# One buffer for the transposed rows, routing factors written twice, and routing weights applied by pairs of token groups

## The chip, the cores and the metric

The kernel runs on one core of one Trainium2 chip. The metric is the device time of one execution in microseconds (us), as the median of several runs.

## What is computed

The reference runs two blocks, one after the other, on 256 tokens of width 1024. The change touches only the last layer of the second block, a mixture of 16,384 tiny experts, and the buffer in which transposed rows are kept for all the large products. Cut to what matters, the layer is:

```
def _peer(h, w_q, subkeys, w_down, w_up):          # h: tokens x 1024
    q = h @ w_q                                    # 8 heads x 2 halves x 128
    s = q . subkeys                                # scores of 128 + 128 half keys for each head
    v, i = top_k(s, 16)                            # the best 16 of each half
    tv, tj = top_k(v0 + v1, 16)                    # the best 16 of the 256 sums
    eidx = 128 * i0 + i1                           # expert number of each choice
    w = softmax(tv)
    a = gelu(h . w_down[eidx])                     # one number per token and chosen expert
    return sum over choices of (w * a) * w_up[eidx]
```

The layer chooses 8 x 16 = 128 experts for each token. Everything is float32.

## The kernel before

Nothing is gathered. The kernel computes all 16,384 expert values for all 256 tokens by dense products, multiplies them with a matrix that holds the routing weight where an expert was chosen and zero elsewhere, and multiplies the result with all of `w_up`. An expert number is 128 * i0 + i1; the i0 from 0 to 63 make the first half (tile `Ga`, called G2 in the code) and those from 64 to 127 the second (tile `Gb`, G1). In both, i1 lies across the partitions.

Products in full precision are made of three passes in a reduced 32-bit form: each operand is split into a high and a low part (`wsplit`: ScalarE, ACT, casts `raw` to `whi`, L239; VectorE, DVE, subtracts to get `wlo`, L240), and `mm3` issues high x high (L244), high x low (L245) and low x high (L246). Weights come in tiles of 128 x 1024, 0.5 MB, through SP's DMA queue, into five `raw` buffers and three pairs of `whi` and `wlo`. The transposed, normalised rows of the tokens, h, stand as a high and a low part of 8 x 256 columns in two buffers, `bh` and `bl` of 2064 elements a partition each (`big_hl`): the high part from element 16 of `bh`, the low part from element 0 of `bl`. Each of four users (two input projections, one merge, the last layer) gets a new generation of them. In the last stage their space is used again for split rows of expert values (`uph` in `bl`, `upl` in `bh`, eight slots).

The last layer runs in this order. PE (TensorE) takes its instructions in the order in which they were written out, as does each other engine.

1. Queries, scores and the top-16 searches (`routing`, `route`), spread between the first products by `drain`. `route(t)` ends, for each tile of 128 tokens, with three transposes and the writing of the factors: `ije` (i0 and i1 for each choice and token) and `wpt` (high and low part of the weight), as 16-bit numbers, 256 tokens wide.
2. First `down` half: 32 calls of `down`, each with two weight tiles of 24 passes of 256 columns, and a gelu by ACT (L1168) into `Ga`.
3. Second `down` half: 32 calls into `Gb`; meanwhile `Ga` is multiplied with the routing weights, 8 tokens (a group) at a time, 32 groups.
4. First `up` half: 64 calls of `upc` on `Ga`, each with 12 passes of 512 columns (L1219); meanwhile `Gb` is multiplied with its routing weights, 32 groups.
5. Second `up` half: 64 calls on `Gb`, without weighing, then the end: residual, norm, output.

A group is prepared on DVE by `make`: R (128 choices x 128 values of i1 for each of 8 tokens, one where equal, L1180), E (the same for 64 values of i0, L1182), and two L (E times high and low part of the weight, L1185). R and L stand in one of two buffers, RL0 and RL1. `weigh` then runs 16 matmuls of 64 columns on PE (two for each token, L1199), which make the dense matrix of weights of that group in PSUM, and DVE multiplies it into the expert values (L1201). `ready` calls `make` for a later group; the loops call `ready` for the next group and then `weigh` for the present one, `spread` over the calls of `down` and `upc`. In R, E and L tokens are interleaved by two, so that the two tokens of a pair lie in adjacent elements: `iota2` holds each number twice, and a matmul reads every second element.

Of the kernel before, what the change touches and what calls it, by code (L numbers as in the profile page):

```python
# [8 lines left out]
F32R = mybir.dt.float32r  # L9
# [161 lines left out]
def _body(ctx, tc, ins, out, dbg, stop):  # L171
# [3 lines left out]
    const = ctx.enter_context(tc.tile_pool(name="const", bufs=1))  # L175
    keep = ctx.enter_context(tc.tile_pool(name="keep", bufs=1))
    raw = ctx.enter_context(tc.tile_pool(name="raw", bufs=5))
    hl = ctx.enter_context(tc.tile_pool(name="hl", bufs=3))
    small = ctx.enter_context(tc.tile_pool(name="small", bufs=4))

# [155 lines left out]
    x2d = [dram.tile([128, 1024], F32, name=f"x2d{t}") for t in range(2)]  # L336
    mod2 = keep.tile([128, 48], F32, name="mod2")
    both = []
    with ExitStack() as c1:
        k1 = c1.enter_context(tc.tile_pool(name="k1", bufs=1))  # L340
        w1 = c1.enter_context(tc.tile_pool(name="w1", bufs=2))
# [17 lines left out]

        def big_hl():  # L360

            both[:] = [keep.tile([128, 2064], F32R, name=n, tag=n) for n in ("bh", "bl")]
            return [m[:, o:o + 2048].rearrange("p (k n) -> p k n", k=8) for m, o in zip(both, (16, 0))]

        scr = k1.tile([128, 256], BF, name="scr")
        scr2 = k1.tile([128, 1024], BF, name="scr2")
# [668 lines left out]
                T.matmul(sp[:, t, f], qhs[h % 2][:, f, t * 128:(t + 1) * 128], sub[:, 2 * h + f], start=True, stop=True)  # L1035
        S.copy(sco[:, h], sp)

    iota2 = k2.tile([128, 128, 2], HF, name="iota2")
    V.tensor_copy(iota2, K["iota"][:, :, None].to_broadcast([128, 128, 2]))
    cst, dst, io16 = [cut([16], HF) for _ in range(3)]  # L1040
    for m, n in ((cst, K["cst"]), (dst, K["dst"]), (io16, K["iota"][:, :16])):
        V.tensor_copy(m, n)
    ge, pr = cut([8, 16, 16], HF), cut([8, 16, 16], HF)
    ije = k2.tile([128, 2, 256], HF, name="ije")
    wpt = k2.tile([128, 2, 256], HF, name="wpt")

    def route(t):

        V.tensor_copy(idf[:, t], idx[:, t])
        v, ix = val[:, t], idf[:, t]  # L1050
        cand = cut([8, NCAND])
        o = 0
        for i0, ni, nj in CAND:
            V.tensor_tensor(cand[:, :, o:o + ni * nj].rearrange("p h (i j) -> p h i j", j=nj),
                            v[:, :, 0, i0:i0 + ni, None].to_broadcast([128, 8, ni, nj]),
                            v[:, :, 1, None, 0:nj].to_broadcast([128, 8, ni, nj]), op=OP.add)
            o += ni * nj
        yield 1.2
        tv, st = [cut([8, 16]) for _ in range(2)]
        pf, d0 = [cut([8, 16], HF) for _ in range(2)]  # L1060
        tp = cut([8, 16], U32)
        wia = cut([3, 8, 16])
        for h in range(8):
            top16(tv[:, h], tp[:, h], cand[:, h], NCAND)
            yield 1.0
        V.tensor_copy(pf, tp)
        V.tensor_sub(st, tv, tv[:, :, 0:1].to_broadcast([128, 8, 16]))
        S.activation(tv, st, AF.Exp)
        V.tensor_copy(d0[:, :, 0:1], ix[:, :, 0, 0:1])
        V.tensor_sub(d0[:, :, 1:], ix[:, :, 0, 1:], ix[:, :, 0, :15])  # L1070
        sh4 = [128, 8, 16, 16]
        f2 = lambda m: m.rearrange("p h s -> p (h s)")
        col = lambda m: f2(m)[:, :, None].to_broadcast([128, 128, 16])
        row = lambda m: m[:, None, :].to_broadcast([128, 128, 16])
        f3 = lambda m: m.rearrange("p h s i -> p (h s) i")
        V.tensor_tensor(f3(ge), col(pf), row(cst), op=OP.is_ge)
        yield 2.8
        sm = small.tile([128, 8], F32, name="sm8")
        V.tensor_reduce(sm, tv, axis=AX.X, op=OP.add)
        V.reciprocal(sm, sm)  # L1080
        V.tensor_mul(wia[:, 0], tv, sm[:, :, None].to_broadcast([128, 8, 16]))
        V.tensor_mul(pr, ge, d0[:, :, None, :].to_broadcast(sh4))
        yield 1.7
        V.tensor_reduce(wia[:, 1], pr, axis=AX.X, op=OP.add)
        yield 2.2
        V.tensor_mul(f3(pr), f3(ge), row(dst))
        yield 1.2
        V.tensor_reduce(st, pr, axis=AX.X, op=OP.add)
        V.tensor_sub(st, pf, st)
        yield 2.4  # L1090
        V.tensor_tensor(f3(ge), col(st), row(io16), op=OP.is_equal)
        yield 2.2
        V.tensor_mul(pr, ge, ix[:, :, 1, None, :].to_broadcast(sh4))
        yield 1.2
        V.tensor_reduce(wia[:, 2], pr, axis=AX.X, op=OP.add)
        yield 2.2
        ps = pb.tile([128, 3, 128], F32, name="tp")
        for i in range(3):
            T.transpose(ps[:, i], wia[:, i].rearrange("p h s -> p (h s)"), ident)
        ts = slice(t * 128, t * 128 + 128)  # L1100
        S.copy(ije[:, :, ts], ps[:, 1:3])
        rem = cut([128])
        S.mul(rem, ps[:, 0], UPSCALE)
        V.tensor_copy(wpt[:, 0, ts], rem)
        V.tensor_sub(wpt[:, 1, ts], rem, wpt[:, 0, ts])
        yield 0.5

    done, budget = [0], [0.0]
# [59 lines left out]
        S.activation(Gh[:, 2 * (c % 32):2 * (c % 32) + 2], ps, AF.Gelu_apprx_tanh)  # L1168

    ng = 8  # L1170
    pair = lambda m, t: m[:, t:t + ng].rearrange("p (a b) -> p a b", b=2)[:, :, None, :]

    def make(hf, t):

        R, L = RL(nth[0] % 2)
        nth[0] += 1
        R = R.rearrange("p (a i b) -> p a i b", a=ng // 2, b=2)
        L = L.rearrange("p (q a i b) -> p q a i b", q=2, a=ng // 2, b=2)
        E = w2.tile([128, ng // 2, 64, 2], HF, name="E", bufs=2)
        V.tensor_tensor(R, iota2[:, None].to_broadcast([128, ng // 2, 128, 2]),  # L1180
                        pair(ije[:, 1], t).to_broadcast([128, ng // 2, 128, 2]), op=OP.is_equal)
        V.tensor_tensor(E, iota2[:, None, hf * 64:hf * 64 + 64].to_broadcast([128, ng // 2, 64, 2]),  # L1182
                        pair(ije[:, 0], t).to_broadcast([128, ng // 2, 64, 2]), op=OP.is_equal)
        for p in range(2):
            V.tensor_tensor(L[:, p], E, pair(wpt[:, p], t).to_broadcast([128, ng // 2, 64, 2]), op=OP.mult)  # L1185
        return R, L

    ahead = []
# [4 lines left out]
    def weigh(Gh):  # L1193

        hf, t, R, L = ahead.pop(0)
        ps = pb.tile([128, ng, 64], F32, name="tp")
        for i in range(ng):
            for p in range(2):
                T.matmul(ps[:, i], R[:, i // 2, :, i % 2], L[:, p, i // 2, :, i % 2], start=p == 0, stop=p == 1)  # L1199
        gv = Gh[:, :, t:t + ng]  # L1200
        V.tensor_mul(gv, gv, ps.rearrange("p t i -> p i t"))  # L1201

# [29 lines left out]
    G1 = k2.tile([128, 64, 256], F32, name="Gb", tag="G1")  # L1232
    two = [w2.tile([128, 2, 1024], HF, name=f"RL{i}") for i in range(2)]
    RL = lambda i: (two[i][:, 0], two[i][:, 1])
    ready(0, 0)
    for c in range(32):
        down(G1, 32 + c)
        for g in spread(32, c, 30) if c < 30 else ():
            if g < 31:
                ready(0, ng * (g + 1))  # L1240
            weigh(G2)
    uph, upl = [m[:, o:o + 2048].rearrange("p (k n) -> p k n", k=8) for m, o in zip(both, (0, 16))]
    ready(1, 0)
    for c in range(64):
        upc(G2, c)
        for g in spread(32, c, 62) if c < 62 else ():
            if g < 31:
                ready(1, ng * (g + 1))
            weigh(G1)
    rs = k2.tile([128, 64 * 256], F32, name="rs2", tag="G2")  # L1250
    used[0] = 0
    xo = cut([2, 1024])
# [61 lines left out]
```

## Time and profile before

| | us |
|---|---|
| median of 3 runs | 1245.26 (1244.03 to 1246.6) |
| the profiled execution | 1246.62 |
| its span, first to last instruction | 1244.8 |
| PE busy | 1190.5 (96%) |
| DVE busy | 959.2 (77%) |
| ACT busy | 585.6 (47%) |

Busy time of PE is made of matmuls that overlap: the next starts while one is still draining, so their durations add up to more than the span, and how fast PE really works is read from the starts of successive matmuls. PEld is the loading of the stationary operand, which runs beside them. In the views, `pa` are the accumulators of `down`, `up` those of `upc`, `tp` the matrix of weights, `RL` the two buffers of R and L, `bh` and `bl` the rows. In square brackets stands the time for which an engine was idle before an instruction, and what ended it.

### The profile page before, as it was taken

The page shows a single profiled execution, that of the slowest core. Times are in us where ns is not written, and L with a number is a line of the kernel's source. Part 1 is how long each engine was busy: PE and PEld are TensorE (multiplying, and loading weights), DVE is VectorE, ACT ScalarE, POOL GpSimd, SP SyncE. Part 2 cuts the span into 40 slices and gives each one's busy share as a digit, 9 for nine tenths or more (in the row PEclk, how much of TensorE's full clock was granted, in tenths as well). Part 3 has the DMA queues.
Part 4 walks back from the last instruction along what each step waited for, and adds up shares of the span by engine and source line. Part 5 has one row for each costly group of instructions (what it writes and reads, how often), then busy time and mean ns, then how long its engine had stood idle before and what let it go on. Part 6 is the DMA issues. An engine that isn't in the chain of part 4 may idle for free. (4 is left out here: it accounts for less than half of the span.)

```text
span 1244.8 us, 22791 instructions
## 1 busy us (share of the span) xinstructions
PE 1190.5 (96%) x8960; PEld 1071.1 (86%) x8960; DVE 959.2 (77%) x2015; ACT 585.6 (47%) x907; POOL 8.7 (1%) x14
## 2 busy tenths in 40 slices
PE   3999999899999899899999999999999999999996
PEld 2998899778788799899999999998777777888884
DVE  6879869768798789997546778778888887666555
ACT  3445547323553545454544444445444444555553
POOL 0000000000000000000000000000000000000001
PEclk9999999999999999999999999999999999999998
DMA  9999846287373444556565555555555556777551
GB/s 320 363 323 317 284 163 198 92 287 253 103 238 118 170 143 165 169 171 202 190 195 175 170 170 170 170 169 171 169 172 179 173 172 237 227 230 238 183 186 51
DMA packets 67451, 245.22 MB, mean 197 GB/s; under 512 B 7504, under 2 KB 8032, under 8 KB 67088
## 3 DMA queue, kind: packets, MB, share of 16 engines
q1 hardware_dynamic: 65136, 236.34, 57.7%
q10 hardware_dynamic: 1440, 4.20, 0.9%
q0 software_dynamic: 768, 3.23, 0.8%
q8 instruction: 70, 1.15, 0.4%
q14 instruction: 37, 0.30, 0.1%
HBM read 241.11 MB, written 2.62 MB: 196 GB/s over the span
## 5 line engine op out<-in xcount | busy, mean ns | idle before, releaser
L240 DVE TENSOR_TENSOR wlo<-raw,whi 128x1024 fp32r<-128x1024 f32 x351 | 427.9, 1222 | 121.8 <-ACT whi L239 120.7
L239 ACT CAST whi<-raw 128x1024 fp32r<-128x1024 f32 x351 | 368.0, 1050 | 326.4 <-PE pa L245 221.7
L246 PE MATMUL pa<-bh,wlo 128*128 128x256 f32 x1120 | 314.6, 281 | 3.7 <-DVE wlo L240 3.5
L244 PE MATMUL pa<-bh,whi 128*128 128x256 f32 x1120 | 317.2, 283 | 0.0
L245 PE MATMUL pa<-bl,whi 128*128 128x256 f32 x1120 | 313.9, 280 | 0.0
L246 PEld LDWEIGHTS pa<-bh,wlo 128*128 128x128 f32 x1120 | 211.7, 189 | 5.0 <-DVE wlo L240 4.9
L245 PEld LDWEIGHTS pa<-bl,whi 128*128 128x128 f32 x1120 | 214.5, 192 | 0.0
L244 PEld LDWEIGHTS pa<-bh,whi 128*128 128x128 f32 x1120 | 211.8, 189 | 0.0
L1219 PE MATMUL up<-whi,bh 128*128 128x512 f32 x508 | 164.1, 403 | 0.0
L1219 PE MATMUL up<-wlo,bh 128*128 128x512 f32 x508 | 160.1, 394 | 0.0
L1219 PE MATMUL up<-whi,bl 128*128 128x512 f32 x508 | 159.8, 394 | 0.0
L1219 PEld LDWEIGHTS up<-wlo,bh 128*128 128x128 f32 x508 | 95.4, 188 | 23.5 <-DVE wlo L240 0.3
L1219 PEld LDWEIGHTS up<-whi,bl 128*128 128x128 f32 x508 | 95.4, 188 | 22.3
L244 PE MATMUL mm<-whi,bh 128*128 128x256 f32 x352 | 102.2, 290 | 11.0 <-ACT whi L239 8.2
L1219 PEld LDWEIGHTS up<-whi,bh 128*128 128x128 f32 x508 | 93.4, 189 | 19.3 <-ACT whi L239 0.2
L245 PE MATMUL mm<-wlo,bh 128*128 128x256 f32 x352 | 101.2, 288 | 2.1 <-DVE wlo L240 2.1
L246 PE MATMUL mm<-whi,bl 128*128 128x256 f32 x352 | 101.1, 287 | 1.1 <-DVE bl L332 1.0
L1185 DVE TENSOR_TENSOR RL<-E,wpt 128x512 f16<-128x512 f16 x128 | 53.9, 422 | 33.7 <-PE tp L1199 33.7
L244 PEld LDWEIGHTS mm<-whi,bh 128*128 128x128 f32 x352 | 67.8, 193 | 13.1 <-ACT whi L239 8.6
L245 PEld LDWEIGHTS mm<-wlo,bh 128*128 128x128 f32 x352 | 67.7, 192 | 3.2 <-DVE wlo L240 2.5
L246 PEld LDWEIGHTS mm<-whi,bl 128*128 128x128 f32 x352 | 67.7, 192 | 2.3 <-DVE bl L332 1.7
L231 ACT CAST bh<-Ga 128x256 fp32r<-128x256 f32 x64 | 25.4, 406 | 86.3 <-PE up L1219 85.1
(400 smaller groups left out, 1709.7 us busy)
## 6 DMA issues: line engine op xcount, KB each, us to landing
raw<-in_wdT_dram SPq DMA_DIRECT2D x128, 512.0 KB, 3.4
raw<-in_wu_dram SPq DMA_DIRECT2D x128, 512.0 KB, 3.5
raw<-in_wada_dram SPq DMA_DIRECT2D x72, 512.0 KB, 4.8
raw<-in_win_dram SPq DMA_DIRECT2D x26, 512.0 KB, 4.5
raw<-in_win1t_dram SPq DMA_DIRECT2D x24, 512.0 KB, 5.0
raw<-in_win1n_dram SPq DMA_DIRECT2D x16, 512.0 KB, 5.2
raw<-in_wout_dram SPq DMA_DIRECT2D x16, 512.0 KB, 3.6
raw<-in_wq_dram SPq DMA_DIRECT2D x12, 512.0 KB, 3.6
```

The source lines that it names most:

```text
L231: S.copy(hi, src)
L239: S.copy(hi, t)
L240: (E or eng()).tensor_tensor(lo, t, hi, op=OP.subtract)
L244: T.matmul(o, a[0], b[0], start=first, stop=False, **kw)
L245: T.matmul(o, a[0], b[1], start=False, stop=False, **kw)
L246: T.matmul(o, a[1], b[0], start=False, stop=last, **kw)
L1185: V.tensor_tensor(L[:, p], E, pair(wpt[:, p], t).to_broadcast([128, ng // 2, 64, 2]), op=OP.mult)
L1219: T.matmul(up[t][d], s_[:, ts], v_[:, d], start=ia == 0 and n == 0, stop=ia == 127 and n == 2)
```

## The change

1. `bh` and `bl` become one buffer of 4128 elements in a pool of its own, `rowp`, which is allocated after `raw` and ahead of the `whi` and `wlo` buffers. h stands in it from element 16 on (high part, then low part), `uph` and `upl` from element 32 on.
2. `ije` and `wpt` hold each value twice, in adjacent elements. `route` writes them with two casts of `ije`, two copies of the high part by ACT, and one subtraction of twice the length on DVE; a cast on DVE goes. `iota2` becomes `iotah`, each number once. R, E and L have each token's values in adjacent elements, and the weigh matmuls read them without a stride. The doubled factors give DVE two adjacent equal elements where there were two tokens. E has one buffer, not two.
3. Two groups are prepared ahead of each loop. Then `pair` weighs two groups in a row and prepares the next two; 16 pairs are spread over the calls where 32 single weighings were.

```diff
+    rowp = ctx.enter_context(tc.tile_pool(name="rowp", bufs=1))
...
+    def parts(o):
+        return [both[0][:, i:i + 2048].rearrange("p (k n) -> p k n", k=8) for i in (o, o + 2048)]
...
-            both[:] = [keep.tile([128, 2064], F32R, name=n, tag=n) for n in ("bh", "bl")]
-            return [m[:, o:o + 2048].rearrange("p (k n) -> p k n", k=8) for m, o in zip(both, (16, 0))]
+            both[:] = [rowp.tile([128, 4128], F32R, name="bhl", tag="bhl")]
+            return parts(16)
...
-    iota2 = k2.tile([128, 128, 2], HF, name="iota2")
-    V.tensor_copy(iota2, K["iota"][:, :, None].to_broadcast([128, 128, 2]))
+    iotah = k2.tile([128, 128], HF, name="iotah")
+    V.tensor_copy(iotah, K["iota"])
...
-    ije = k2.tile([128, 2, 256], HF, name="ije")
-    wpt = k2.tile([128, 2, 256], HF, name="wpt")
+    ije = k2.tile([128, 2, 256, 2], HF, name="ije")
+    wpt = k2.tile([128, 2, 256, 2], HF, name="wpt")
...
-        S.copy(ije[:, :, ts], ps[:, 1:3])
         rem = cut([128])
         S.mul(rem, ps[:, 0], UPSCALE)
-        V.tensor_copy(wpt[:, 0, ts], rem)
-        V.tensor_sub(wpt[:, 1, ts], rem, wpt[:, 0, ts])
+        for b in range(2):
+            S.copy(ije[:, :, ts, b], ps[:, 1:3])
+            S.copy(wpt[:, 0, ts, b], rem)
+        V.tensor_sub(wpt[:, 1, ts], rem[:, :, None].to_broadcast([128, 128, 2]), wpt[:, 0, ts])
...
-    pair = lambda m, t: m[:, t:t + ng].rearrange("p (a b) -> p a b", b=2)[:, :, None, :]
+    twice = lambda m, t, w: m[:, t:t + ng, None, :].to_broadcast([128, ng, w // 2, 2])
...
-        R = R.rearrange("p (a i b) -> p a i b", a=ng // 2, b=2)
-        L = L.rearrange("p (q a i b) -> p q a i b", q=2, a=ng // 2, b=2)
-        E = w2.tile([128, ng // 2, 64, 2], HF, name="E", bufs=2)
-        V.tensor_tensor(R, iota2[:, None].to_broadcast([128, ng // 2, 128, 2]),
-                        pair(ije[:, 1], t).to_broadcast([128, ng // 2, 128, 2]), op=OP.is_equal)
-        V.tensor_tensor(E, iota2[:, None, hf * 64:hf * 64 + 64].to_broadcast([128, ng // 2, 64, 2]),
-                        pair(ije[:, 0], t).to_broadcast([128, ng // 2, 64, 2]), op=OP.is_equal)
+        two_ = lambda m: m.rearrange("p t (i b) -> p t i b", b=2)
+        R = R.rearrange("p (t i) -> p t i", t=ng)
+        L = L.rearrange("p (q t i) -> p q t i", q=2, t=ng)
+        E = w2.tile([128, ng, 64], HF, name="E")
+        V.tensor_tensor(two_(R), two_(iotah[:, None].to_broadcast([128, ng, 128])), twice(ije[:, 1], t, 128), op=OP.is_equal)
+        V.tensor_tensor(two_(E), two_(iotah[:, None, hf * 64:hf * 64 + 64].to_broadcast([128, ng, 64])),
+                        twice(ije[:, 0], t, 64), op=OP.is_equal)
         for p in range(2):
-            V.tensor_tensor(L[:, p], E, pair(wpt[:, p], t).to_broadcast([128, ng // 2, 64, 2]), op=OP.mult)
+            V.tensor_tensor(two_(L[:, p]), two_(E), twice(wpt[:, p], t, 64), op=OP.mult)
...
-                T.matmul(ps[:, i], R[:, i // 2, :, i % 2], L[:, p, i // 2, :, i % 2], start=p == 0, stop=p == 1)
+                T.matmul(ps[:, i], R[:, i], L[:, p, i], start=p == 0, stop=p == 1)
...
-    ready(0, 0)
+    def pair(Gh, hf, n):
+        for _ in range(2):
+            weigh(Gh)
+        for g in (n + 2, n + 3):
+            if g < 32:
+                ready(hf, ng * g)
+    for g in range(2):
+        ready(0, ng * g)
     for c in range(32):
         down(G1, 32 + c)
-        for g in spread(32, c, 30) if c < 30 else ():
-            if g < 31:
-                ready(0, ng * (g + 1))
-            weigh(G2)
-    uph, upl = [m[:, o:o + 2048].rearrange("p (k n) -> p k n", k=8) for m, o in zip(both, (0, 16))]
-    ready(1, 0)
+        for n in spread(16, c, 30) if c < 30 else ():
+            pair(G2, 0, 2 * n)
+    uph, upl = parts(32)
+    for g in range(2):
+        ready(1, ng * g)
     for c in range(64):
         upc(G2, c)
-        for g in spread(32, c, 62) if c < 62 else ():
-            if g < 31:
-                ready(1, ng * (g + 1))
-            weigh(G1)
+        for n in spread(16, c, 62) if c < 62 else ():
+            pair(G1, 1, 2 * n)
```

## Rows read from the trace of the kernel before

**Rows 1.** The page: busy us of PE, share of the span, instructions.
```profile
PE 1190.5 (96%) x8960; PEld 1071.1 (86%) x8960; DVE 959.2 (77%) x2015; ACT 585.6 (47%) x907; POOL 8.7 (1%) x14
```

**Rows 2.** Busy time by stretch: second `down` half, then first `up` half.
```profile
657.00:855.40 198.40, 198.40 (x2052) 197.09 (x2051) 149.13 (x226) 84.73 (x102) 0.00 (x0) 1.00 0.55 171
855.40:1049.30 193.90, 193.90 (x1270) 154.70 (x1269) 167.44 (x279) 92.19 (x130) 2.10 (x4) 1.00 0.56 182
```

**Rows 3.** PE in order of time (start, length): one `down` between two single weighings.
```profile
669.48 0.28 PE L245 MATMUL pa<-bl,whi 128*128 128x256 f32 x1
...
674.78 0.28 PE L245 MATMUL pa<-bl,whi 128*128 128x256 f32 x1
...
675.02 0.66 PE L1199 MATMUL tp<-RL 128*128 128x64 f16 x16
675.51 0.36 PE L244 MATMUL pa<-bh,whi 128*128 128x256 f32 x1
675.71 0.28 PE L245 MATMUL pa<-bl,whi 128*128 128x256 f32 x1
```

**Rows 4.** PE in order of time: two weighings in a row, and the `down` behind.
```profile
749.82 1.14 PE L1199 MATMUL tp<-RL 128*128 128x64 f16 x32
750.79 0.36 PE L244 MATMUL pa<-bh,whi 128*128 128x256 f32 x1
751.00 0.28 PE L245 MATMUL pa<-bl,whi 128*128 128x256 f32 x1
...
756.11 0.28 PE L245 MATMUL pa<-bl,whi 128*128 128x256 f32 x1
```

**Rows 5.** PE by line (count, busy us, mean ns): 669.6-749.6, 763.0-844.0, 751.0-762.3, 844.9-855.2.
```profile
L245 PE MATMUL pa<-bl,whi 128*128 128x256 f32 x208 | 58.4, 281 | 0.0
...
L246 PE MATMUL pa<-bh,wlo 128*128 128x256 f32 x208 | 58.4, 281 | 0.0
...
L245 PE MATMUL pa<-bl,whi 128*128 128x256 f32 x32 | 8.8, 276 | 0.0
...
L245 PE MATMUL pa<-bl,whi 128*128 128x256 f32 x31 | 8.6, 276 | 0.0
```

**Rows 6.** ACT in order of time: two gelus in a row, first `down` half.
```profile
652.71 0.59 ACT L1168 ACTIVATE Ga<-pa 128x512 f32<-128x512 f32 x1
...
658.15 0.59 ACT L1168 ACTIVATE Ga<-pa 128x512 f32<-128x512 f32 x1
```

**Rows 7.** PE in order of time: `up` with weighings, then two plain calls.
```profile
867.12 0.66 PE L1199 MATMUL tp<-RL 128*128 128x64 f16 x16
...
873.27 0.66 PE L1199 MATMUL tp<-RL 128*128 128x64 f16 x16
...
1091.31 0.64 PE L1219 MATMUL up<-whi,bh 128*128 128x512 f32 x2
...
1094.11 0.64 PE L1219 MATMUL up<-whi,bh 128*128 128x512 f32 x2
```

**Rows 8.** DVE in order of time, around the double weighing.
```profile
750.48 0.43 DVE L1185 TENSOR_TENSOR RL<-E,wpt 128x512 f16<-128x512 f16 x1 [1.10 <-PE tp L1199]
750.83 0.68 DVE L1201 TENSOR_TENSOR Ga<-Ga,tp 128x512 f32<-128x512 f32 x1
751.42 0.69 DVE L1180 TENSOR_TENSOR RL<-iota,ije 128x1024 f16<-128x1024 f16 x1
...
754.23 2.36 DVE L240 TENSOR_TENSOR wlo<-raw,whi 128x1024 fp32r<-128x1024 f32 x2
756.51 0.76 DVE L1182 TENSOR_TENSOR E<-iota,ije 128x512 f16<-128x512 f16 x2
```

**Rows 9.** DVE in order of time, first `up` half.
```profile
867.39 0.42 DVE L232 TENSOR_TENSOR bl<-Ga,bh 128x256 fp32r<-128x256 f32 x1 [0.56 <-PE up L1219]
```

**Rows 10.** ACT in order of time, end of `route` for the first tile.
```profile
598.35 0.29 ACT L1103 ACTIVATE rs<-tp 128x128 f32<-128x128 f32 x1
599.72 1.05 ACT L239 CAST whi<-raw 128x1024 fp32r<-128x1024 f32 x1 [1.08 <-PE pa L245]
```

## The prediction

> **What bounds the kernel now.** I read the page first: TensorE (PE) is busy for 96% of the span [rows 1]; then the table by stretches. The change touches the expert part, in which PE never rests: busy 198.40 of 198.40 us in the second half of the `down` products, with `weigh` for the first 64 experts of a row between them, and 193.90 of 193.90 in the `up` products that carry the other weighing [rows 2]. VectorE (DVE) works 149 and 167 us of these, and the granted clock is 1.00 in both, which is its level of 2.4 GHz. So nothing that DVE, ACT or a queue saves there can shorten the span; only the spacing of PE's own passes counts, and a wait that the change brings in.
>
> So I read the starts of the passes, not their durations, which overlap. In a `down` run after one weighing (16 short matmuls) a 256-column pass starts every (674.78 - 669.48)/45 = 0.1178 us [rows 3]. In the run after the one place where two weighings already stand back to back (32 matmuls) it is (756.11 - 751.00)/45 = 0.1136 us [rows 4]: same line, tiles, clock, other level. The modelled duration follows the spacing (281 against 276 ns), and so shows the level of long stretches: 281 in 13 runs of 48 passes after single weighings (208 passes of that line, 16 to a run), 281 again in 13 more after 763 us, 276 in the two runs from 751 to 762 us and 276 in the run behind the second double weighing at 844 us [rows 5]. Without any weighing, at 652 to 658 us, one `down` of 48 passes takes 5.44 us, or 0.113 [rows 6]. The level is thus set where the stream is restarted, and holds until it is broken again. Both doubles led to the fast level; 26 runs after singles stand at the slow one.
>
> **The weighing in pairs.** It takes nothing out: 64 weighings of 16 matmuls stay, now two in a row, 16 pairs to each half.
> - Level of the `down` runs: 26 runs x 48 passes x (117.8 - 113.6 = 4.2 ns) = 5.3 us, if every pair restarts the stream as the two doubles did [rows 3 to 5]. I take that, since these are the only rows of 32 matmuls in a row. Its other end is zero, or a loss of 0.8 us if the four fast `down`s (192 passes x 4.2 ns) are lost too.
> - Changeover: a single weighing takes 675.51 - 675.02 = 0.49 us, and the first pass behind it 0.20 instead of 0.12, so 0.08 us is the price of the break [rows 3]; two in a row take 0.97 and then 0.21 [rows 4]. There are 30 breaks now and 16 after: 14 x 0.08 = 1.2 us.
> - `up` half: two `up`s with a weighing take 873.27 - 867.12 = 6.15 us, two plain ones 2 x (1094.11 - 1091.31) = 5.60, so a weighing costs 0.55 [rows 7]. A pair costs 0.55 + 0.48 = 1.03, and 16 pairs save 16 x 0.07 = 1.1 us.
>
> Contiguous operands for the weigh matmuls (they are every second element now): 16 in 0.49 us is 30 ns each for 64 columns, 27 ns at one column per cycle of 2.4 GHz. So between nothing and 1024 x 3 ns = 3 us of gain; a loss isn't shown by any row, though a block that ends at another instant could choose another level, which is counted above. I take nothing.
>
> **What DVE has to do at once.** `ready` is called after both weighings and writes the two RL buffers that these read, so both makes wait for the pair. Queued behind them on DVE are the `wlo` subtractions, and for those waits PE. A make keeps its four operations and element counts, with two adjacent 16-bit elements innermost as before, so I cost it at nothing. The double at 750 us shows the pile: from 750.83 to 754.23 two multiplies, two R and three L, 3.40 us, with 1.10 us of idle DVE ahead, and two E later in 0.76 [rows 8]; together 4.2 us, and then 1.2 for `wlo`: 5.4 us. At the end of the pair PE has two split tiles ready: 2 x 24 x 0.1136 = 5.45 us in the down half and 2 x 2.80 = 5.60 in the up half. Hidden, with 0.1 and 0.2 us to spare; the part of the pile that starts while the second weighing still runs (0.48 us) adds to this. Without that cover it costs what the third rival says. The E buffer goes from two to one: E and L follow one another on DVE anyway, nothing. Where two pairs stand in adjacent `down`s (twice) I allow 0.1 us each.
>
> **Routing factors, written twice.** Per token tile ACT gets three more copies and DVE loses a small cast, while its subtraction doubles. With the 0.29 us of the copy there, 3 x 0.3 = 0.9 us on ACT, whose next `whi` cast starts after 1.08 us of waiting for PE [rows 10]: covered. The DVE subtraction now waits for ACT's copies; behind it in the queue stand makes and one `wlo` whose tile PE wants two `down` halves later. Zero, at most 2 x 0.5 us. The DMA queue of SP and POOL's are passed by none of this.
>
> **One buffer for the rows.** A new generation of the buffer is released by the last reader of either half, not by each half's own: one pass of 0.12 us, at most twice on the path, 0.2 us. The rows of the `up` half now begin 16 elements later than those of `down`, so the first casts wait for the next block's passes too, four passes or 0.45 us, while 18 of the last 24 passes are still ahead of PE: hidden. Where the buffer lies can't be priced from the trace: both levels appear at one place. Bounds: in the first `down` half, 32 x 48 passes that may change level, up to 6.5 us; I keep half of that, 3.2, on either side. For `up` the best would be twice the fast level (227 ns against 2.80/12 = 233), 1536 x 6 ns = 9 us of gain, the worst twice the slow one (235.6), 3.6 us. I take zero, since the two halves of the old buffer, at different places, give one spacing.
>
> **Sum.** -5.3 - 1.2 - 1.1 + 0.2 + 0.2 = -7.2 us. Against the profiled execution's own 1246.62 us (span 1244.8 and 1.8 around it) that is 1239.4; the median is 1245.26, 1.36 below that execution, which leaves **1238.0 us**.
>
> **Rivals.**
> - *Mixed levels.* A restart does not always choose alike: after the double at 750 us a single one gave the fast level once more (the second of the two runs up to 762 us), then the next gave the slow [rows 5]. If every second pair lands fast: -2.65 - 2.3 + 0.4 = -4.6, **1240.7 us**. For it: no pair in the trace follows passes at the fast level. Chance 0.20.
> - *The level does not follow the pairing.* Then the changeovers alone come back and the four `down`s at the fast level may go: -2.3 + 0.4 + 0.8 = -1.1, **1244.2 us**. Against it: two doubles out of two. The Trainium skill (TensorE: Matmul & The Clock Gate, section Back-to-back issue gap) gives the gap as columns over clock plus a constant, 109 ns for 256 columns, with no place for what ran before. By that rule there would be one level and this rival would hold; the trace has two, at 113.6 and 117.8 ns, so the measurement speaks against it here. Chance 0.20.
> - *The pile on DVE stops PE.* Place: the `up` half, where short subtractions of the rows (0.42 us each, one waiting 0.56 us for PE as it is [rows 9]) share the queue. If two of them stand between the makes and `wlo`, 5.4 + 0.84 - 5.6 = 0.64 us per pair, 16 pairs: 10 us. On top of the sum that is +3, **1248.3 us**, and with the second rival up to 1254. It decides as soon as more than 0.2 us of other work stands ahead of `wlo`. Against it: the double at 750 us cost PE nothing, and DVE idles ahead of each weighing. Chance 0.10.
> - *The new views cost DVE its rate.* L1201, on 32-bit data, does 512 elements in 0.68 us where an L takes 0.42 and an R of 1024 0.69. At its rate a make of 2560 elements takes 3.4 us rather than 1.95, 1.4 more: 32 x 1.4 = 46 us in the `up` half, where DVE has 193.9 - 167.4 = 26.5 us free [rows 2, 8]: +20, 1258 us. Nothing in the diff takes away the adjacent pair; chance 0.03. The rest, 0.02, is a faster spacing of the `up` passes.
>
> **How the numbers follow.** The forecast has 0.45. The range goes from 1230 (the sum, with 3.2 us of levels in the first half and most of the gain of the short matmuls or some of `up`) to 1247 (the second rival with 3 us of levels against it); it leaves out the two last cases and the dear part of the third. A measurement of this kernel can tell about 0.2%, 2.5 us, from no change. Faster by more: 0.45 + 0.20 + 0.02, less a little for levels elsewhere, 0.65. Within: the second rival and what was taken off, 0.23. Slower: the third and fourth, 0.12.
>
> **What would show it.** In the profile after: pairs of 32 short matmuls, and behind each of them L245 at 276 ns rather than 281 and `down`s 5.44 us long; the stretch from the first weighing to the first `up` some 6.5 us shorter; the `up` stretch 1 us shorter with PE busy throughout. PE waits for `wlo` behind a pair show the third rival; makes longer than 0.69 and 0.42 us the fourth. Levels that change in the first `down` half, or `up` passes off 233 ns, would make the sum wrong from a side that the trace doesn't price.

## The result, and the profile after

The changed kernel takes 1229.55 us (1228.47 to 1231.78) against 1245.93 for the kernel before on the same chips: a ratio of 0.9866, 95% interval 0.984 to 0.9893. That is a gain of 16.4 us where 7.2 were forecast, and just outside the range of 1230 to 1247. Its profiled execution took 1229.27 us, with a span of 1227.5.

One correction first, since steps below rest on it. The text ahead of the prediction exchanges the places of two parts: the code `zip(both, (0, 16))` puts `uph` into `bh` from element 0 and `upl` into `bl` from element 16, and [rows 9] show the low part written to `bl`. The expectations of e5, e6, e9 and e13 that speak of the layout or the addresses of the kernel before share this misreading, and the 233 ns that e3 expects at element 16 go with it; e17 has the true ones.

The page of the changed kernel, to be read against [rows 1]: busy us of PE, share of the span, instructions.

```profile
PE 1172.0 (95%) x8960; PEld 1063.5 (87%) x8960; DVE 955.3 (78%) x2013; ACT 587.0 (48%) x913; POOL 8.6 (1%) x14
```

Busy time by stretch, each cut at the first weighing, the first `up` and the 65th `up`; the kernel before, then the changed one (stretch, its length, busy us of PE, PEld, DVE, ACT, POOL, granted clock, DMA share, GB/s).

```profile
0.00:662.60 662.60, 619.73 (x4898) 576.38 (x4899) 521.36 (x1342) 316.27 (x547) 1.47 (x6) 0.99 0.63 212
662.60:855.40 192.80, 192.80 (x2002) 191.52 (x2002) 146.68 (x224) 82.13 (x99) 0.00 (x0) 1.00 0.55 170
855.40:1052.10 196.70, 196.70 (x1282) 156.96 (x1281) 170.11 (x284) 93.76 (x132) 2.10 (x4) 1.00 0.56 182
1052.10:1232.90 180.80, 180.80 (x784) 146.23 (x783) 114.24 (x148) 90.51 (x125) 2.58 (x2) 1.00 0.60 192
```
```profile
0.00:668.30 668.30, 624.54 (x4945) 580.82 (x4946) 523.50 (x1341) 320.46 (x556) 1.46 (x6) 0.99 0.63 212
668.30:848.20 179.90, 179.90 (x1954) 179.36 (x1953) 142.94 (x222) 79.49 (x96) 0.00 (x0) 1.00 0.58 176
848.20:1039.50 191.30, 191.30 (x1283) 157.75 (x1282) 168.23 (x286) 93.69 (x132) 2.08 (x4) 1.00 0.60 188
1039.50:1215.40 175.90, 175.90 (x784) 145.62 (x783) 113.66 (x148) 90.48 (x125) 2.57 (x2) 1.00 0.62 197
```

With pairs the first weighing stands one `down` later (48 passes, 5.4 us), so that `down` moves from the second stretch into the first. Taken back, the gains are: second `down` half 192.8 - 179.9 - 5.4 = 7.5 us, first `up` half 5.4, second `up` half 4.9. The first stretch is 0.3 us longer than before and what follows the last `up` 0.2 longer. Together that is 17.3, the difference of the two spans. PE is busy throughout the expert part in both, at a granted clock of 1.00, so all of the gain is spacing of passes, as the prediction read it. But 4.9 us come from the second `up` half, in which nothing is weighed and no term of the prediction lay.

PE in order of time in the changed kernel, a pair and the `down` behind it (start, length), to be read against [rows 3, 4]:

```profile
668.28 1.11 PE L1205 MATMUL tp<-RL 128*128 128x64 f16 x32
669.23 0.37 PE L245 MATMUL pa<-bhl,whi 128*128 128x256 f32 x1
669.43 0.28 PE L246 MATMUL pa<-bhl,whi 128*128 128x256 f32 x1
...
674.54 0.28 PE L246 MATMUL pa<-bhl,whi 128*128 128x256 f32 x1
```

The pass behind the pair starts after 0.95 us, and then (674.54 - 669.43)/45 = 0.1136 us a pass: the quick level. It holds behind every pair. PE by line from the first weighing to the first `up` (count, busy us, mean ns of one), changed kernel:

```profile
L246 PE MATMUL pa<-bhl,whi 128*128 128x256 f32 x481 | 132.9, 276 | 0.0
```

This is the 276 of [rows 5], now for the whole half. A plain `up` call, against [rows 7]: of its 12 passes four read `wlo`, in two groups of two, so from one such group to the next but one is one call.

```profile
1185.93 0.62 PE L1225 MATMUL up<-wlo,bhl 128*128 128x512 f32 x2
...
1188.65 0.62 PE L1225 MATMUL up<-wlo,bhl 128*128 128x512 f32 x2
```

2.72 us, or 226.7 ns a pass, where it was 2.80 and 233.3. DVE around the pair, in square brackets what it waited for, against [rows 8]:

```profile
668.93 0.42 DVE L1191 TENSOR_TENSOR RL<-E,wpt 128x512 f16<-128x512 f16 x1 [0.98 <-PE tp L1205]
669.27 1.28 DVE L1207 TENSOR_TENSOR Ga<-Ga,tp 128x512 f32<-128x512 f32 x2
670.47 0.69 DVE L1187 TENSOR_TENSOR RL<-iotah,ije 128x1024 f16<-128x1024 f16 x1
671.07 0.42 DVE L1191 TENSOR_TENSOR RL<-E,wpt 128x512 f16<-128x512 f16 x1
671.41 0.69 DVE L1187 TENSOR_TENSOR RL<-iotah,ije 128x1024 f16<-128x1024 f16 x1
672.01 0.42 DVE L1188 TENSOR_TENSOR E<-iotah,ije 128x512 f16<-128x512 f16 x1
672.34 1.22 DVE L241 TENSOR_TENSOR wlo<-raw,whi 128x1024 fp32r<-128x1024 f32 x1
```

R still takes 0.69 us and L and E 0.42; the first `wlo` starts 672.34 - 669.27 = 3.07 us after the multiplies, less than the 4.2 of the pile, since the last two L stand behind it. And ACT at the end of `route` for the first tile, against [rows 10]:

```profile
598.38 0.27 ACT L1107 ACTIVATE rs<-tp 128x128 f32<-128x128 f32 x1
...
599.33 0.37 ACT L1110 CAST wpt<-rs 128x128 f16<-128x128 f32 x1
600.01 1.05 ACT L240 CAST whi<-raw 128x1024 fp32r<-128x1024 f32 x1 [0.32 <-PE pa L246]
```

The next `whi` cast still waits for PE, 0.32 us of it left.

### The profile page after: what moved, and what is told of

Read it like the earlier page. It is cut to its first block, busy times and chain, and to the rows that moved or that the text cites. A ratio compares the mean times of both kernels' runs of the same rounds, so it can differ in the third digit from the quotient of the medians.

```text
span 1227.5 us, 22802 instructions
## 1 busy us (share of the span) xinstructions
PE 1172.0 (95%) x8960; PEld 1063.5 (87%) x8960; DVE 955.3 (78%) x2013; ACT 587.0 (48%) x913; POOL 8.6 (1%) x14
## 5 line engine op out<-in xcount | busy, mean ns | idle before, releaser
L247 PE MATMUL pa<-bhl,wlo 128*128 128x256 f32 x1120 | 312.2, 279 | 4.0 <-DVE wlo L241 4.0
L245 PE MATMUL pa<-bhl,whi 128*128 128x256 f32 x1120 | 313.6, 280 | 0.0
L246 PE MATMUL pa<-bhl,whi 128*128 128x256 f32 x1120 | 311.7, 278 | 0.0
L1225 PE MATMUL up<-whi,bhl 128*128 128x512 f32 x1016 | 277.5, 391 | 0.0
L1225 PEld LDWEIGHTS up<-whi,bhl 128*128 128x128 f32 x1016 | 189.3, 188 | 38.8 <-ACT whi L240 0.2
L247 PEld LDWEIGHTS pa<-bhl,wlo 128*128 128x128 f32 x1120 | 211.8, 189 | 5.4 <-DVE wlo L241 5.2
L246 PEld LDWEIGHTS pa<-bhl,whi 128*128 128x128 f32 x1120 | 212.0, 189 | 0.0
L245 PEld LDWEIGHTS pa<-bhl,whi 128*128 128x128 f32 x1120 | 211.4, 189 | 0.0
L1225 PE MATMUL up<-wlo,bhl 128*128 128x512 f32 x508 | 157.8, 390 | 0.0
L245 PE MATMUL mm<-whi,bhl 128*128 128x256 f32 x352 | 101.3, 288 | 10.7 <-ACT whi L240 7.5
L246 PE MATMUL mm<-wlo,bhl 128*128 128x256 f32 x352 | 100.8, 286 | 3.5 <-DVE wlo L241 3.5
L247 PE MATMUL mm<-whi,bhl 128*128 128x256 f32 x352 | 100.4, 285 | 1.0 <-DVE bhl L333 1.0
L245 PEld LDWEIGHTS mm<-whi,bhl 128*128 128x128 f32 x352 | 67.2, 191 | 12.8 <-ACT whi L240 7.9
L247 PEld LDWEIGHTS mm<-whi,bhl 128*128 128x128 f32 x352 | 66.9, 190 | 2.2 <-DVE bhl L333 1.6
```

The lines of the kernel that those rows point to most:

```text
L245: T.matmul(o, a[0], b[0], start=first, stop=False, **kw)
L246: T.matmul(o, a[0], b[1], start=False, stop=False, **kw)
L247: T.matmul(o, a[1], b[0], start=False, stop=last, **kw)
L1225: T.matmul(up[t][d], s_[:, ts], v_[:, d], start=ia == 0 and n == 0, stop=ia == 127 and n == 2)
```

## Experiments: one part at a time

**e1: the kernel before with pairs only** (`two_of` does what `pair` does in the changed kernel; the same in the `up` loop).

```diff
-    ready(0, 0)
+    for g in range(2):
+        ready(0, ng * g)
...
-        for g in spread(32, c, 30) if c < 30 else ():
-            if g < 31:
-                ready(0, ng * (g + 1))
-            weigh(G2)
+        for n in spread(16, c, 30) if c < 30 else ():
+            two_of(G2, 0, 2 * n)
```

> The kernel before with the weighing in pairs alone; old buffers, interleaved factors and two E buffers stay. Theory P (the way the stream is restarted sets both spacings): `down` runs behind the pairs at 113.5 ns a pass and 276 ns duration, and the `up` passes at 226.7 ns as in the changed kernel, about 1229 to 1231 us. Theory A (the spacing of the `up` passes is set by where the split rows lie against the split weights, that of the `down` passes by the pairs): `down` at 113.5, `up` at 233 as before, 1246 - 7 = about 1239 us.

1240.54 us, ratio 0.9948 (0.993 to 0.9966). Its two halves, `down` from the first weighing and first `up`:

```profile
671.10:852.00 180.90, 180.90 (x1954) 180.33 (x1953) 142.86 (x222) 79.60 (x96) 0.00 (x0) 1.00 0.56 175
852.00:1047.80 195.80, 195.80 (x1283) 158.76 (x1282) 168.20 (x285) 93.67 (x132) 2.09 (x4) 1.00 0.60 183
```

192.8 - 5.4 - 180.9 = 6.5 us in the `down` half and 0.9 in the `up` half: the forecast's 6.5 (5.3 + 1.2) and 1.1. One of the 16 pairs did not do what was forecast: behind the first, the two `down`s (96 passes) stood at 117.8 ns, behind the other 15 at 113.5. The plain `up` call stays at 2.80 us. The total shows less than 7.4 because the first stretch, ahead of any pair, came out 671.1 - 662.6 - 5.4 = 3.1 us longer. By the starts of the passes, 91% of those of the first `down` half lay at the slow level in e1, 34% in the kernel before, and that half took 188.0 us instead of 185.2, though nothing ahead of it was edited. That is the chance term of 3.2 us.

**e2: the kernel before with the one buffer only** (first part of the change).

```diff
-            both[:] = [keep.tile([128, 2064], F32R, name=n, tag=n) for n in ("bh", "bl")]
-            return [m[:, o:o + 2048].rearrange("p (k n) -> p k n", k=8) for m, o in zip(both, (16, 0))]
+            both[:] = [rowp.tile([128, 4128], F32R, name="bhl", tag="bhl")]
+            return parts(16)
...
-    uph, upl = [m[:, o:o + 2048].rearrange("p (k n) -> p k n", k=8) for m, o in zip(both, (0, 16))]
+    uph, upl = parts(32)
```

> The kernel before with the one buffer alone (rows of `down` from element 16, rows of `up` from element 32, in front of the split weights); single weighings and interleaved factors stay. Theory A: `up` passes at 226.7 ns, `down` runs behind single weighings at 117.8 as before, 1246 - 9 = about 1237 us. Theory P: `up` at 233 and `down` at 117.8, no change from 1246 us.

1239.99 us, ratio 0.9954 (0.9938 to 0.9969). The `down` half from the first weighing is unchanged, the `up` halves take it all (second `down` half, the two `up` halves; then plain calls, PE in order of time):

```profile
663.40:856.20 192.80, 192.80 (x2002) 191.52 (x2002) 146.67 (x224) 82.04 (x99) 0.00 (x0) 1.00 0.55 170
856.20:1049.30 193.10, 193.10 (x1283) 156.84 (x1282) 170.00 (x284) 93.76 (x132) 2.09 (x4) 1.00 0.57 186
1049.30:1225.20 175.90, 175.90 (x785) 145.58 (x783) 113.67 (x147) 90.47 (x125) 2.58 (x2) 1.00 0.62 197
```
```profile
1186.20 0.61 PE L1224 MATMUL up<-wlo,bhl 128*128 128x512 f32 x2
...
1188.92 0.61 PE L1224 MATMUL up<-wlo,bhl 128*128 128x512 f32 x2
```

2.72 us a call without pairs or new factors, 3.6 us less in the first `up` half and 4.9 in the second. This is the gain that the forecast lacked, and it belongs to the buffer.

**e7: the kernel before with the contiguous factors only** (the second part of the change whole, single weighings).

```diff
-                T.matmul(ps[:, i], R[:, i // 2, :, i % 2], L[:, p, i // 2, :, i % 2], start=p == 0, stop=p == 1)
+                T.matmul(ps[:, i], R[:, i], L[:, p, i], start=p == 0, stop=p == 1)
```

> The kernel before with the factors written twice and the contiguous operands alone. Short matmuls start every 31.0 ns in the kernel before and in the pairs and buffer runs, every 29.5 in the changed kernel. Theory: contiguous operands are the cause, 1024 x 1.5 = 1.5 us less, 1246.3 - 1.5 = about 1245 us, `down` runs behind single weighings at 117.8 still. Rival: the end of a weighing falls at another instant and the `down` runs go to 113.5, then about 1239 us. A third: makes get slower on DVE (over 0.69 and 0.42 us) or their order does, and PE waits, over 1247 us.

1243.64 us, ratio 0.9971 (0.9955 to 0.9987). PE around a single weighing:

```profile
672.72 0.64 PE L1200 MATMUL tp<-RL 128*128 128x64 f16 x16
673.20 0.37 PE L244 MATMUL pa<-bh,whi 128*128 128x256 f32 x1
673.40 0.28 PE L245 MATMUL pa<-bl,whi 128*128 128x256 f32 x1
...
678.51 0.28 PE L245 MATMUL pa<-bl,whi 128*128 128x256 f32 x1
```

(678.51 - 673.40)/45 = 0.1136: the quick level, behind single weighings. So the number of short matmuls isn't what decides. With the second part of the change, all 30 breaks of this half lead to the quick level, singles too; in the kernel before 27 of its 28 singles led to the slow one. e7 changes the writing of the factors along with the strides, so the stride alone isn't shown to be what chooses. By their starts the short matmuls take 29.8 ns each instead of 31.0. From first weighing to first `up` it is 187.0 us instead of 192.8; the first `up` half stays at 196.7. The total gains less than these 5.8 us, because the first weighing of the profiled execution came at 666.7 us, 4.1 later than in the kernel before.

**e8: the changed kernel with single weighings** (the loops of the kernel before).

```diff
-        for n in spread(16, c, 30) if c < 30 else ():
-            pair(G2, 0, 2 * n)
+        for g in spread(32, c, 30) if c < 30 else ():
+            if g < 31:
+                ready(0, ng * (g + 1))
+            weigh(G2)
```

> The changed kernel with single weighings as before. Theory pairs (32 short matmuls in a row restart the stream at the quick spacing, 16 do not): `down` runs at 117.8 ns in the second half, +5.3 and 14 more breaks +1.2 and `up` +1 us, 1229.5 + 7.5 = about 1237 us. Rival (the contiguous operands or the layout do it): `down` runs stay at 113.5, +2 us, about 1231.5 us.

1233.62 us, ratio 0.9903 (0.9879 to 0.9926). `down` half and `up` half:

```profile
664.00:851.00 187.00, 187.00 (x2003) 185.97 (x2002) 146.78 (x224) 82.11 (x99) 0.00 (x0) 1.00 0.52 175
851.00:1044.50 193.50, 193.50 (x1283) 156.32 (x1282) 169.79 (x285) 93.65 (x132) 2.08 (x4) 1.00 0.53 185
```

Inside the changed kernel the pairs are worth 187.0 - 5.4 - 179.9 = 1.7 and 193.5 - 191.3 = 2.2 us, 3.9 together. In the `down` half these are changeovers alone, since the level is the quick one either way; in the `up` half the passes between the breaks also stand 228.6 ns apart with singles and 227.6 with pairs, 0.7 of the 2.2 us. The parts are thus not additive: pairs and factors each buy the same 5 us of level.

## Experiments: what of the buffer quickens the `up` passes

From here on most kernels were timed once (e5, e6, e9 and e11 to e18; e3 and e4 four times, e10 ten times), so the argument goes by the spacing of the passes in the trace, and the totals stand beside it.

The programs' addresses tell the places. The split weight tiles stand at the same bytes in all kernels here, 4096 apart. Call *offset* the bytes by which split rows stand ahead of the next address that is a multiple of 4096 from those tiles. Element 32 of the new buffer has offset 0, element 24 has 32, element 16 has 64, element 8 has 96, element 0 has 128. In the kernel before `uph` has 128 and `upl` 0; after, both have 0. The rows of `down` and of the projections have 64 in both kernels.

**Place and order.** e4 puts the new buffer into the place of the old (20,480 bytes lower, 5 x 4096; the pool `rowp` goes); e5 exchanges high and low part.

```diff
e4
-            both[:] = [rowp.tile([128, 4128], F32R, name="bhl", tag="bhl")]
+            both[:] = [keep.tile([128, 4128], F32R, name="bhl", tag="bhl")]
e5
-    uph, upl = parts(32)
+    upl, uph = parts(32)
```

> The changed kernel with its one buffer back in the old place, ahead of the raw tiles and 20,480 bytes (five times 4096) further from the split weights; offsets 16 and 32 stay. Offset as the cause: `up` at 226.7 ns, no change from 1229.5 us. Place as the cause: 233 ns, about 1239 us.

> The changed kernel with high and low part of the `up` rows exchanged: the low part at element 32, the high part 2048 elements further, as they lay in the old buffers (high part above the low one). So far the `up` half has shown three levels: 2800 ns for 12 passes in the kernel before, 2750 with the rows at element 16 and the high part first, 2720 at element 32 with the high part first. Theory order (which part comes first makes the step that the offset does not): about 2750 to 2770 ns here, 1229.5 + 4 to 6 = about 1234 us. Theory place (the old pair of buffers was too far or too near): 2720, 1229.5 us.

1230.47 us (ratio 0.9874, 0.9848 to 0.9901) and 1229.4; the plain call takes 2.72 us in both. Neither the place nor the order of the parts matters, nor that there is one buffer in a pool of its own.

**Offset, both parts alike.** e6 is e3 with the parts exchanged, e9 and e13 are these two in the old place; e11 has `parts(24)`, e12 `parts(0)`.

```diff
e3
-    uph, upl = parts(32)
+    uph, upl = parts(16)
```

> The changed kernel with the rows of `up` from element 16, like those of `down`, so that they begin 16,448 bytes ahead of the first split weight tile and not 16,384 (64 bytes off). Theory A with the offset as its cause: `up` passes back at 233 ns, 1229.5 + 9 = about 1239 us. If the buffer's place in front of the weights is the cause, or the pairs: 226.7 ns stays, 1229.5 us.

> The changed kernel with the `up` rows at element 16 and the parts exchanged: the layout of the kernel before in all but its distance from the split weights (a multiple of 4096 bytes). If order and offset together are the cause: 2800 ns for 12 passes as before, 1229.5 + 10 = about 1239 us. If the distance matters: less than 2800.

> The changed kernel with its buffer in the old place and the `up` rows at element 16: these rows then have the very addresses of the kernel before (parts exchanged, which made no difference). Up to now: element 32 gives 2720 ns for 12 passes in either place, element 16 gives 2750 in the new place. Theory place-with-offset (an offset that is 64 bytes off costs more when the rows lie further away): 2800 here, 1229.5 + 10 = 1239.5 us. Theory new operands or pairs took part of it: 2750, about 1231 us.

> The changed kernel with the `up` rows at the very addresses and in the very order of the kernel before (old place, element 16, high part above the low one). Kernels with these addresses and the old code show 2800 ns for 12 passes, the same offset with the new code 2747 three times. Theory address (this one combination of place and order is dear): 2800, about 1239 us. Theory restart (at an offset of 64 bytes two levels are possible, as 113.5 and 117.8 are for `down`, and what runs ahead of the `up` half chooses): 2747, about 1231 us.

> The changed kernel with the `up` rows at element 24, 32 bytes off a multiple of 4096 from the split weights. Theory offset in fine steps: a level between 2720 and 2750 ns for 12 passes, about 1230.5 us. Theory whole lines of 64 bytes: at one of the two known levels, 2720 or 2750.

> The changed kernel with the `up` rows at element 0, 128 bytes off a multiple of 4096. If the distance counts in multiples of 128 bytes: 2720 ns for 12 passes, 1229.5 us. If only a whole multiple of 4096 is quick: 2750 or 2800, 1231 to 1239 us.

| | offset of both | plain `up` call, us | total, us |
|---|---|---|---|
| after | 0 | 2.72 | 1229.55 |
| e11 | 32 | 2.80 | 1234.17 |
| e3 | 64 | 2.75 | 1229.74 |
| e6, e9, e13 | 64 | 2.75 | 1231.51, 1231.85, 1231.76 |
| e12 | 128 | 2.78 to 2.80 | 1239.98 |

The spacing goes with the offset, in either place and order. e11 fits neither of its two theories: 32 bytes off is as slow as 128. That e9 and e13 came out at 2.75, as their second theories had it, tells nothing about the kernel before, whose offsets they do not have. The totals carry besides what happens ahead of the first `up`, which these edits leave alone: e11 gets there at 844.1 us, e3 at 845.9, the changed kernel at 848.2, e12 at 850.9. PE in order of time, e3 and e11:

```profile
1186.14 0.62 PE L1225 MATMUL up<-wlo,bhl 128*128 128x512 f32 x2
...
1188.89 0.62 PE L1225 MATMUL up<-wlo,bhl 128*128 128x512 f32 x2
```
```profile
1186.09 0.63 PE L1225 MATMUL up<-wlo,bhl 128*128 128x512 f32 x2
...
1188.89 0.63 PE L1225 MATMUL up<-wlo,bhl 128*128 128x512 f32 x2
```

**The offsets of the kernel before, inside the changed one.** e17 gives `uph` offset 128 and `upl` 0; e18 turns them round.

```diff
-    uph, upl = parts(32)
+    uph, upl = [both[0][:, i:i + 2048].rearrange("p (k n) -> p k n", k=8) for i in (0, 2080)]
```

> The changed kernel with the high split rows of the up half from element 0 and the low ones from element 2080 of the one buffer. Its program's addresses put the high rows 128 bytes off a multiple of 4096 from the split weight tiles and the low rows on one. This is what the program of the kernel before has too: there the high rows stand in bh from element 0 and the low ones in bl from element 16 (what earlier expectations called the layout of the kernel before had the two exchanged). Theory that the offset of the rows against the split weights sets the spacing of the up passes: 12 passes of a plain up call in 2.80 us, as before, 1536 x 6.6 ns = 10 us more than the changed kernel, 1239 us. Rival, that it is the place of the buffer or its being one: 2.72 us and 1229 to 1231 us.

> The changed kernel with the low split rows of the up half from element 0 (128 bytes off) and the high ones from element 2080 (0 off). The high rows serve 8 of 12 passes of an up call, the low ones 4. If each pass's spacing follows the offset of its own rows: 8 x 226.7 + 4 x 232.5 = 2.744 us, 1229.5 + 3 = 1232.5 us, and the run before this would have 4 x 226.7 + 8 x 232.5 = 2.767, not 2.80. If one part that is off sets the spacing of the whole call: 2.79 to 2.80 us, 1239 us, in both.

e17: 1233.24 us; e18: 1238.14. A plain call of e17, and its two `up` halves; then the first `up` half of e18:

```profile
1186.60 0.63 PE L1225 MATMUL up<-wlo,bhl 128*128 128x512 f32 x2
...
1189.40 0.63 PE L1225 MATMUL up<-wlo,bhl 128*128 128x512 f32 x2
```
```profile
843.40:1038.80 195.40, 195.40 (x1283) 158.30 (x1282) 168.18 (x285) 93.58 (x132) 2.08 (x4) 1.00 0.56 184
1038.80:1219.60 180.80, 180.80 (x785) 146.20 (x783) 114.28 (x148) 90.45 (x125) 2.57 (x2) 1.00 0.58 192
```
```profile
849.30:1044.20 194.90, 194.90 (x1282) 157.79 (x1281) 168.16 (x285) 93.51 (x132) 2.09 (x4) 1.00 0.54 184
```

2.80 us again, in the new place and the one buffer, and 195.4 + 180.8 against 191.3 + 175.9: 9.0 us dearer than the changed kernel, the offsets alone undone. The total of e17 missed its expected 1239 for another reason: its first weighing came at 663.4 us, 4.9 earlier. At 410 us it was 0.6 us ahead. From 410 to 440 us, in the queries and scores, PE was granted 0.89 in the changed kernel (in two stretches of 3.4 us, at 416.4 and 433.4 us, it had the lower level, 1.2 GHz) and 1.00 in e17, where it did 209 matmuls instead of 174. Ahead of the first fall, from 410 to 416.4 us, it had been busy alike, 4.70 and 4.66 us (changed kernel, then e17):

```profile
410.00:440.00 30.00, 24.74 (x174) 23.24 (x173) 19.33 (x71) 13.85 (x27) 1.26 (x2) 0.89 0.46 159
```
```profile
410.00:440.00 30.00, 26.08 (x209) 24.59 (x208) 23.13 (x90) 15.17 (x27) 1.26 (x2) 1.00 0.48 169
```

e18's call takes 2.79 us, not the 2.744 of a price pass by pass: one part that stands off slows the whole call, though the other has offset 0. That the new place and the one buffer by themselves quicken `up` is ruled out by e17.

## Experiments: the same offset in `down`

The rows of `down` and of the projections are moved, to element 32 (e10), 24 (e14), 8 (e15) and 0 (e16); the `up` rows stay at offset 0.

```diff
e10
-            return parts(16)
+            return parts(32)
```

> The changed kernel with all rows at element 32, those of the projections and of `down` too, so that they begin 16,384 bytes ahead of the first split weights. Theory offset (streams that begin at a whole multiple of 4096 bytes from each other run at the quick spacing): the projections with the rows as the stationary operand go from 117.8 to 113.5 ns, 1056 passes, at most 4.5 us where PE sets the time, and the first `down` half keeps 113.5 throughout, 1500 x 1.6 = 2.4 us: 1223 to 1227 us. Rival (what suits `up` doesn't suit `down`, whose stationary operand is the weights): `down` at 117.8 in both halves, +9 us, about 1238 us. If offset matters for 512-column passes alone: 1229.5 us.

> The changed kernel with the rows of the projections and of `down` at element 24 (32 bytes off a multiple of 4096 from the split weights); `up` rows stay at element 32. At 64 bytes `down` passes start every 113.5 or 117.8 ns, at 0 every 119.9. Theory: the spacing of 256-column passes has an offset that suits it, as that of 512 columns has (0 bytes), and 64 is one that allows the quick spacing; at 32 bytes 113 to 120, from 1227 (quick throughout) to 1243 us. If only 64 bytes allows it: 117.8 or more, over 1236 us.

> As the run with element 24, with the rows of the projections and of `down` at element 8 (96 bytes off). Quick throughout: about 1227 us; only the slow spacing: over 1236 us.

> As the run with element 24, with the rows of the projections and of `down` at element 0 (128 bytes off). Quick throughout: about 1227 us; only the slow spacing: over 1236 us. If the offset counted modulo 128 bytes it would behave like the run with element 32: 119.9 ns, about 1246 us.

| | offset of h | `down` pass, second half, ns | total, us |
|---|---|---|---|
| after | 64 | 113.5 | 1229.55 |
| e10 | 0 | 119.9 | 1246.28 |
| e14 | 32 | 118.3 | 1240.97 |
| e15 | 96 | 117.4 | 1241.78 |
| e16 | 128 | 119.0 | 1243.52 |

e14 to e16 ran on a chip on which the kernel before took 1251.87 us and e13, with the rows of `down` at offset 64, 1231.76. e10 met none of its expectations: it is slower than its dearest, 1238. e10 against the kernel before is 0.9987 (0.9969 to 1.0005): with pairs, factors and quick `up` calls it has given everything back. PE by line in e10, first weighing to first `up`, against the 276 above:

```profile
L246 PE MATMUL pa<-bhl,whi 128*128 128x256 f32 x481 | 136.0, 283 | 0.0
```

The best offset for `up` (0), where the rows are the stationary operand, is the worst tried for `down`, where they are the moving one; the elements 16 and 32 of the change are the best tried for each.

## Why the prediction was wrong, point by point

- **What bounds the kernel**: right. PE stayed busy through the expert part and all of the gain is spacing.
- **Level behind pairs, -5.3, and changeovers, -1.2 and -1.1**: right for the part done alone (e1: 6.5 and 0.9; the 14 x 0.08 of the changeovers is 1.1, not 1.2). The reason was too narrow: e7 and e8 reach the same level with single weighings once the second part of the change is in. That the level is set where the stream is restarted stands: in the first `down` half an unbroken run of some 380 passes lay at 113.3 ns in the kernel before and at 117.8 in e1. That it takes 32 short matmuls doesn't, nor that 32 strided ones always do it (e1's first pair).
- **Contiguous operands, 0 within 0 to 3 us of gain**: the size was about right beside the pairs, 180.9 - 179.9 = 1.0 us in the `down` half, of which 96 x 4.3 ns = 0.4 are e1's first run at the slow level. What was missed is that this part of the change brings the quick level by itself.
- **The buffer's place, 0 within 9 of gain and 3.6 of loss**: this is the step that failed. The bound was right (8.5 us in e2, 9.0 between e17 and the changed kernel); the value taken, nothing, was not. It was argued from "the two halves of the old buffer, at different places, give one spacing" (by the starts in plain calls, 234 ns with rows in `bh` and 232 in `bl`), which took nearly equal spacing as a sign that places don't matter. e18 shows why it isn't: a call takes the spacing of its worse part, so two parts at offsets 128 and 0 look alike. That the old parts stood at different offsets and the new ones at one could have been worked out from the code; that one offset is quicker could not, since the trace of the kernel before shows `up` at one pair of offsets only. The range then held only "some of `up`" at its low end. With this term the sum, -7.2 - 8.5, gives 1229.6. That this is the measured time to 0.1 us is luck: the profiled executions differ by 17.3 us and not 15.7.
- **First `down` half, 3.2 us by chance**: right in size for a loss, not shown for a gain. e1 has 91% of its passes at the slow level and takes 2.8 us more, though it changes nothing ahead of them; e9 has 6% and takes 185.1 us, no less than the 185.2 of the kernel before with 34%. The changed kernel has 37%, and its first stretch is 0.3 us longer.
- **Buffer waits and adjacent pairs, +0.2 each; the doubled factors on ACT**: from the first weighing on PE is busy throughout, so no wait behind adjacent pairs is seen. The new generation of the rows and the factors lie in the first stretch, where PE also rests for other reasons; it is 0.3 us longer in all, and no run shows the two terms apart.
- **Rivals.** In the changed kernel the mixed levels and the level that doesn't follow pairing fell: all 16 pairs led to 113.5 ns. With strided operands a little of the mixture is there: 15 of 16 pairs in e1. The Trainium skill's rule (TensorE: Matmul & The Clock Gate, section Back-to-back issue gap), columns over clock plus 2.5 ns, which it calls the gap of an isolated matmul, gives one value for 256 columns; the traces have three, 113.5, 117.8 and 119.9 ns, for the same shape at the granted clock 1.00. The pile on DVE cost nothing: PE never waited behind a pair, and the first `wlo` came 3.07 us behind the multiplies, not 4.2. The DVE rate didn't change.

What stays open: why the offset acts. The weights stood at the same bytes in all kernels, so it isn't shown whether the offset against them or the absolute address counts, nor with what period; moves by 4096 bytes and multiples changed nothing. What about the restart chooses between 113.5 and 117.8 ns is open too: e7 narrows it to the second part of the change, not to the stride alone.

## What to carry to other kernels

Where PE is the bound and never waits, read the starts of successive passes by operand pair, and look up the addresses of both operands: a shift of the rows by 32 to 128 bytes changed the spacing by 1 to 6% here, and for `up` alone it was worth 9 us, more than the restructured weighing. Try the offsets for each product apart, since the best for one was the worst for the other. An edit that only moves a buffer can have a price on such an engine; if the trace can't give its sign, let the range hold both ends of its bound.

## What was not expected of the hardware

- On the mean of a call, 512-column passes stood 226.7 ns apart at offset 0, 229 at 64 and 232 to 233.3 at 32 and 128; 256-column passes 113.5 or 117.8 at 64 and 117.4 to 119.9 elsewhere, all at the granted clock 1.00. The Trainium skill (TensorE: Matmul & The Clock Gate, section Step-by-step: what each phase is for) says that the two operands come through two independent read ports, so that loading the next stationary operand takes no bandwidth from the running matmul; it names no effect of addresses, and these runs show one.
- A stream of equal passes holds one of two spacings, 113.5 or 117.8 ns, until it is broken. Behind sixteen short matmuls with strided operands it was the slow one in 27 of 28 cases of the kernel before; behind sixteen with contiguous operands, and factors written twice, the quick one in all 28 (e7).
